# Low parts of the weights in the heads by an accumulating transfer instead of a VectorE subtraction

## The chip, the cores and the metric

The kernel runs on one core of a Trainium2 chip. The metric is the device time of one execution in microseconds (us). Five engines work side by side and meet through semaphores: TensorE (PE in the profile, with PEld for its weight loads), VectorE (DVE), ScalarE (ACT), GpSimd (POOL) and SyncE (SP). Transfers are issued by an engine's queue and carried out by 16 DMA engines; SP issues the plain weight loads, POOL issues those that add to what already lies in the destination.

## The reference, cut to what matters

The reference is a trunk of two residual layers on 512 tokens of width 1024. Each layer normalises x, multiplies it by one wide weight matrix, runs three token mixers on the pieces, gates and merges them and applies an output projection:

```python
for l in range(DEPTH):                                   # DEPTH = 2
    h = rms_norm(x, norm_gain[l])
    proj = jnp.einsum('bld,dn->bln', h, w_in[l])         # 1024 x 8448
    (qa, fa_f, fa_b, ia, za, ub, vb, zb, qc, kc, vc, zc,
     g_a, g_b, g_c) = jnp.split(proj, split_at, axis=-1)
    ya = hgrn2(qa, fa_f, fa_b, ia) ... * silu(za)        # 4 heads, both directions
    yb = spatial_gating(gelu(ub), gelu(vb), ...) * silu(zb)
    yc = window_attention(rope(qc), rope(kc), vc, ...) * silu(zc)
    merged = sigmoid(g_a) * (ya @ w_branch_a) + ...      # three branches
    x = x + merged @ w_out[l]
```

Everything is float32. The kernel computes a float32 product with TensorE's rounded type (fp32r) by splitting each operand into a high part (the value rounded to fp32r) and a low part (value minus high part), and adding three products: high x high, low x high, high x low. Every weight therefore needs a high and a low tile before TensorE can use it.

## The kernel before, in words

**Weights.** All weights are packed into tiles of 128 x 1024 float32 (512 KB). `weight_plan` gives 86 of them per layer in the order in which they are used: 14 tiles for the attention projections and the value IA of the recurrence; then the heads, which take tiles 14 to 41; then 36 tiles for the merges and 8 for the output projection. In layer 2 the same place has a number 92 higher among the operands, because the output projection makes 14 operands, some of them sums, from its 8 tiles, so that a layer has 92. This text writes #26 for operand 26. The stretch of the heads is, in this order: for head 0 the tiles QA, FF, FB, ZA (#14 to #17); the same for head 1 (#18 to #21); the four tiles of VB (#22 to #25); UB and ZB of group 0 and of group 1 (#26 to #29); heads 2 and 3 (#30 to #37); UB and ZB of groups 2 and 3 (#38 to #41).

**How a tile becomes an operand.** `w_load_to` loads it into one of four raw buffers (tag `wr`) through the SP queue (L207). `w_conv_to` takes a high buffer (tag `wh`, five of them) and a low buffer (tag `wl`, four of them) and calls `split`: ACT copies the raw tile into the high one, which rounds it (the CAST of L235), and DVE subtracts the high tile from the raw one into the low one (the TENSOR_TENSOR of L236). Only then can the raw buffer be loaded again. `w_ahead(n)` converts up to n operands ahead of the one in use and keeps the loads N_RAW ahead. In the output projection some raw tiles get a second tile added by a transfer from POOL (L209 and L230, `accum_op=ALU.add`); these are the only accumulating transfers.

**Who reads the operands.** A block of TensorE makes one 128 x 512 result in PSUM. `t_block` (L489) takes one tile with the weights as the stationary side: eight times the three products, so 24 matmuls that read the high tile first and the low tile third. `nat_block` (L442) has the activations stationary and reads four tiles at once: the VB stage runs over four blocks of 128 tokens, and each block reads all four VB tiles (units 0 to 3). So the four low buffers are all taken by VB's units until the last block of tokens has read them; the first low buffer to come free is unit 0's. (In the trace a t_block's matmul is written `pm<-hth,wl`, whichever side is stationary.)

**What sets the order.** The kernel is written as a main line of such blocks with side work (the recurrence `gla`, the attention, the spatial gate) put in between by `advance`. A scheduler then orders the instructions of each engine by its own model of their durations; only what is pinned stays in the order of the program. Each engine runs its list in order, and an instruction that waits holds up those behind it on its engine. The attention's score tiles pass through DRAM by POOL's transfers L781 (out) and L782 (back); gelu on VB's and UB's results is ACT's L1010 (Square) and L1013 (Sigmoid) with DVE's L1011, L1012 and L1014; L879 is an ACT copy inside the recurrence; L1031 is the side matmul in `ln_v` that multiplies a matrix of ones with the spatial weights.

Of the kernel before, what the change touches and what calls it, by code (L numbers as in the profile page):

```python
# [16 lines left out]
AF = mybir.ActivationFunctionType  # L17
ALU = mybir.AluOpType
# [16 lines left out]
C_QA, C_FF, C_FB, C_IA, C_ZA = 0, 512, 1024, 1536, 2048  # L35
# [14 lines left out]
def weight_plan():  # L50

    plan = []

    def nat(c):
        for i in range(4):
            plan.append(("n", c, i))

    nat(C_QC)
    for g in range(2):
        plan.append(("z", g))  # L60
    for i in range(2):
        plan.append(("k", C_KV, i))
    for g in range(2, 4):
        plan.append(("z", g))
    nat(C_IA)
    for h in range(H):
        for c in (C_QA, C_FF, C_FB, C_ZA):
            plan.append(("t", c + P * h))
        if h == 1:
            nat(C_VB)  # L70
        if h % 2 == 1:
            for g in (h - 1, h):
                plan.append(("t", C_UB + P * g))
                plan.append(("t", C_ZB + P * g))
    for br, cg in ((2, C_GC), (1, C_GB), (0, C_GA)):
        for n, j in enumerate(MERGE):
            plan.append(("t", cg + P * j))
            if n % 2 == 0:
                plan.append(("b", br, j, MERGE[n + 1]))

    for r, u in ((0, 0), (1, 0), (1, 1), (0, 1)):
        for i in range(2):
            plan.append(("o", u, 2 * r + i))
    return plan


PLAN = weight_plan()
NW = len(PLAN)

LOAD_SUM = {l * NW + NW - 2 + i: l * NW + NW - 4 + i for l in range(L) for i in range(2)}  # L90


def operand_plan():


    ops = []
    for l in range(L):
        ops += [(l * NW + k, None, None) for k in range(NW - 8)]
        x, w, z, y = ([l * NW + NW - 8 + 2 * q + i for i in range(2)] for q in range(4))
        t = [("sum", l, i) for i in range(2)]  # L100
        for a, b, c in ((x, y, None), (w, None, None), (x, None, (t, z)), (t, w, None), (z, None, None), (y, None, None), (t, None, None)):
            ops += [(a[i], b and b[i], c and (c[0][i], c[1][i])) for i in range(2)]
    return ops


OPERANDS = operand_plan()
# [3 lines left out]
def pack_weights(w_in, wa, wb, wc, wo):  # L110
    out = np.empty((L * NW, P, 1024), w_in.dtype)
    for l in range(L):
        wi = w_in[l].reshape(KT, P, -1)

        wcp = wc[l].reshape(2, 4, 64, D).transpose(1, 0, 2, 3)
        br = [w.reshape(4, P, D) for w in (wa[l], wb[l], wcp)]
        w2 = wo[l].reshape(KT, P, D)
        for i, it in enumerate(PLAN):
            if it[0] == "t":
                blk = wi[:, :, it[1] : it[1] + P]  # L120
            elif it[0] == "z":
                g = C_ZC + it[1] * 64
                blk = np.concatenate([wi[:, :, g : g + 64], wi[:, :, g + 256 : g + 320]], axis=2)
            elif it[0] == "k":
                blk = wi[4 * it[2] : 4 * it[2] + 4, :, it[1] : it[1] + 256]
            elif it[0] == "n":
                blk = wi[2 * it[2] : 2 * it[2] + 2, :, it[1] : it[1] + 512]
            elif it[0] == "b":
                w = br[it[1]]
                blk = np.concatenate([w[:, :, c * P : (c + 1) * P] for c in it[2:]], axis=0)  # L130
            else:
                blk = w2[2 * it[2] : 2 * it[2] + 2, :, it[1] * 512 : it[1] * 512 + 512]
            out[l * NW + i] = blk.transpose(1, 0, 2).reshape(P, 1024)
    return out
# [26 lines left out]
def build(nc, tc, cp, wp, sb, pp, dp, x, wpk, brow, gainb, pvec, wsp, trig, amask, imask, out):  # L161
    V, S, G, E = nc.vector, nc.scalar, nc.gpsimd, nc.tensor
# [4 lines left out]
    def nm(s):  # L167
        cnt[0] += 1
        return f"{s}_{cnt[0]}"

    def m4(shape=(P, 1024), dt=F32):
        return sb.tile(list(shape), dt, name=nm("m4"), tag="m4", bufs=N_M4)
# [23 lines left out]
    def w_load_to(i):  # L196
        while wstate["loaded"] < min(i, L * NW):
            k = wstate["loaded"]

            q = k % NW - (NW - 8)  # L200
            if q in (0, 1):
                if q == 0:
                    hold["t"] = sb.tile([P, 3, 1024], F32, name=nm("hold"), tag="scores", bufs=1)
                t = hold["t"][:, q]
            else:
                t = wp.tile([P, 1024], F32, name=nm("wr"), tag="wr", bufs=N_RAW)
            pin(nc.sync.dma_start(t, wpk[k]))  # L207
            if k in LOAD_SUM:
                G.dma_start(t, wpk[LOAD_SUM[k]], accum_op=ALU.add)  # L209
            raws[k] = t  # L210
            wstate["loaded"] += 1

    def raw(k):
        if k not in raws:
            w_load_to(k + 1)
        return raws[k]

    def w_conv_to(i, order=free, eng=V):
        while wstate["conv"] < min(i, len(OPERANDS)):
            n = wstate["conv"]  # L220
            k, add, form = OPERANDS[n]
            r = raw(k)
            if form:
                raws[form[0]] = hold["t"][:, 2] if form[0][2] == 0 else m4()
                G.tensor_tensor(raws[form[0]], r, raw(form[1]), ALU.add)
            hi = wp.tile([P, 1024], F32R, name=nm("wh"), tag="wh", bufs=N_HI)
            lo = wp.tile([P, 1024], F32R, name=nm("wl"), tag="wl", bufs=N_LO)
            split(r, hi, lo, order, eng)
            if add is not None:
                G.dma_start(r, wpk[add], accum_op=ALU.add)  # L230
            his[n], los[n] = hi, lo
            wstate["conv"] += 1

    def split(src, hi_dst, lo_dst, order=free, eng=V):
        order(S.copy(hi_dst, src))  # L235
        order(eng.tensor_tensor(lo_dst, src, hi_dst.bitcast(F32), ALU.subtract))  # L236

    wi = [0]

    def w_next():  # L240
        i = wi[0]
        wi[0] += 1
        w_conv_to(i + 1)
        return his[i], los[i]

    def w_ahead(n, eng=V):
        w_conv_to(wi[0] + n, eng=eng)
        n = min(wi[0] + n, len(OPERANDS) - 1)
        if n % NOPS >= NOPS - 14:
            w_load_to((n // NOPS + 1) * NW)  # L250
        else:
            w_load_to(OPERANDS[n][0] + N_RAW)
# [121 lines left out]
    s0 = pre.squares([0], 0, D, pin)  # L374
    pre.stats([0], s0, pin)
    w_conv_to(1, pin)
    pre.scale([0], pin, LO)
    pre.scale([0], pin, HI)
# [184 lines left out]
    for l in range(L):  # L563
# [27 lines left out]
        def nat_units(handler, us, before=None, two=False, passes=IN_ORDER):  # L591
            un = [w_next() for _ in range(4)]
            for tb in range(NT):
                if before is not None:
                    before(tb)
                if two and tb < 2:
                    if tb == 1:
                        pos = nat_two(un, *hN, (0, 1), lambda n: advance(us / 2))
                        for i in range(2):
                            handler(i, pos[i])  # L600
                            advance(us / 2)
                    continue
                po = nat_block(un, *hN, tb, lambda: advance(us), passes if tb == 0 else IN_ORDER)
                if tb == NT - 1:
                    w_ahead(2)
                handler(tb, po)
                advance(us)

        def nat_kv(handler, us):
            un = (w_next(), w_next())  # L610
            for pair in range(2):
                po = nat_pair(un, *hN, pair, lambda: advance(us))
                if pair == 1:
                    w_ahead(1)
                handler(pair, po)
                advance(us)

        def main_t():
            po = t_block(*w_next(), 0, *hT, KT, lambda: advance(2.6))
            w_ahead(1)  # L620
            return po
# [711 lines left out]
```

## Time and profile before

| | |
|---|---|
| time, median of 3 runs | 1082.95 us (1082.73 to 1083.31) |
| time of the profiled execution | 1083.25 us |
| its span in the trace | 1081.5 us |
| TensorE (PE) busy | 1073.6 us, 99% of the span |
| VectorE (DVE) busy | 743.6 us, 69% |
| ScalarE (ACT) busy | 439.9 us, 41% |
| GpSimd (POOL) busy | 75.8 us, 7% |
| read from HBM | 122.73 MB |
| heads of layer 1 in the trace | 89 to 294 us |
| heads of layer 2 in the trace | 621 to 825 us |

The span runs from the first to the last instruction in the trace; 1.75 us of the execution's time lie outside it. An engine is busy while an instruction of it runs; a queue's issuing work counts as busy for POOL only. Times on a row are from the span's start.

### The profile page before, as it was taken

To read this page: it belongs to the slowest core of one execution; us is meant where nothing else is said; L and a number is where in the kernel's file an instruction comes from. 1 tells how busy PE (TensorE), PEld (TensorE's weight loads), DVE (VectorE), ACT (ScalarE), POOL (GpSimd) and SP (SyncE) were. 2 spreads that over 40 slices of the span, in tenths; PEclk is the share of its full clock that TensorE was granted. 3 is DMA by queue.
4 is the path that set the end of the run, shared out by engine and by line. 5 is a ranking of instruction groups with operands and counts; after the bars stand their busy time and mean duration, and the time that the engine had idled before them with its cause. 6 is when DMAs were issued, how large, how long until landed. Compare 5 with 4: busy or idle time off the path is not lost.

```text
span 1081.5 us, 17209 instructions
## 1 busy us (share of the span) xinstructions
PE 1073.6 (99%) x6904; PEld 883.9 (82%) x6904; DVE 743.6 (69%) x1453; ACT 439.9 (41%) x673; POOL 75.8 (7%) x110
## 2 busy tenths in 40 slices
PE   9999999999999999999999999999999999999998
PEld 8888877878788888888879888687878888888886
DVE  6974799887974634356887578998688645335485
ACT  5354655354423423224534366554343223222342
POOL 0220111000000000001102201000000000000030
PEclk9999999999999999999999999999999999999999
DMA  8463454253223233244937345434413213323364
GB/s 307 151 200 108 156 176 157 76 193 108 75 64 98 78 98 98 95 138 91 299 127 229 122 157 191 140 118 153 140 43 96 63 71 101 98 79 120 115 178 132
DMA packets 40896, 141.67 MB, mean 131 GB/s; under 512 B 5104, under 2 KB 5616, under 8 KB 40816
## 3 DMA queue, kind: packets, MB, share of 16 engines
q1 hardware_dynamic: 28656, 100.20, 28.6%
q0 software_dynamic: 10432, 36.18, 11.9%
q10 hardware_dynamic: 1728, 4.20, 1.0%
q8 instruction: 54, 0.88, 0.3%
q14 instruction: 26, 0.21, 0.1%
HBM read 122.73 MB, written 17.83 MB: 130 GB/s over the span
## 4 chain that ended last, share of the span: by engine, by line
PE 97%; DVE 1%; ACT 1%; DMA 1%; issue 0%; SPq 0%; ACTq 0%
PE pm L489 65%; PE pm L442 11%; PE ps L1181 4%; PE pm L1181 4%; PE pm L477 2%; PE ps L795 2%; PE ps L890 1%; PE ps L980 1%; PE ps L745 1%; PE ps L746 1%; PE ps L987 1%; PE ps L970 1%; PE ps L939 1%; PE ps L1045 1%; DMA wr<-in_wpk 1%; PE ps L915 1%
## 5 line engine op out<-in xcount | busy, mean ns | idle before, releaser
L235 ACT CAST wh<-wr 128x1024 fp32r<-128x1024 f32 x168 | 176.4, 1053 | 389.8 <-PE pm L489 178.6
L489 PE MATMUL pm<-hth,wh 128*128 128x512 f32 x832 | 330.0, 397 | 0.0
L489 PE MATMUL pm<-htl,wh 128*128 128x512 f32 x832 | 325.1, 391 | 0.0
L489 PE MATMUL pm<-hth,wl 128*128 128x512 f32 x832 | 325.0, 391 | 0.0
L236 DVE TENSOR_TENSOR wl<-wr,wh 128x1024 fp32r<-128x1024 f32 x168 | 204.1, 1221 | 160.9 <-PE pm L489 103.9
L489 PEld LDWEIGHTS pm<-hth,wh 128*128 128x128 f32 x832 | 156.4, 188 | 33.9 <-issue 2.9
L489 PEld LDWEIGHTS pm<-hth,wl 128*128 128x128 f32 x832 | 156.3, 188 | 32.9
L489 PEld LDWEIGHTS pm<-htl,wh 128*128 128x128 f32 x832 | 156.5, 188 | 31.6 <-issue 1.3
L489 PE MATMUL pm<-m,wh 128*128 128x512 f32 x384 | 118.7, 391 | 0.0
L489 PEld LDWEIGHTS pm<-m,wh 128*128 128x128 f32 x384 | 71.8, 188 | 14.7
L948 DVE TENSOR_TENSOR m<-m,f 128x512 f32<-128x512 f32 x112 | 73.7, 687 | 7.2 <-PE ps L915 3.5
L442 PE MATMUL pm<-wh,hth 128*128 128x512 f32 x192 | 74.7, 398 | 0.6 <-ACT hth L235 0.5
L489 PE MATMUL pm<-m,wl 128*128 128x512 f32 x192 | 74.8, 390 | 0.0
L442 PE MATMUL pm<-wh,htl 128*128 128x512 f32 x192 | 73.6, 393 | 0.2 <-DVE htl L236 0.2
L442 PE MATMUL pm<-wl,hth 128*128 128x512 f32 x192 | 73.2, 392 | 0.0
L1124 DVE TENSOR_TENSOR t<-pm,t 128x512 f32<-128x512 f32 x32 | 22.1, 691 | 42.1 <-PE pm L489 42.1
L442 PEld LDWEIGHTS pm<-wh,hth 128*128 128x128 f32 x192 | 36.0, 188 | 10.2 <-ACT hth L235 1.3
L442 PEld LDWEIGHTS pm<-wh,htl 128*128 128x128 f32 x192 | 36.1, 188 | 7.7 <-DVE htl L236 0.5
L442 PEld LDWEIGHTS pm<-wl,hth 128*128 128x128 f32 x192 | 36.1, 188 | 7.5
L489 PEld LDWEIGHTS pm<-m,wl 128*128 128x128 f32 x192 | 36.1, 188 | 7.5
L230 POOL DMA_DIRECT2D hold<-in_wpk x6 | 5.3, 885 | 503.1 <-DVE wl L236 254.6
L879 ACT COPY t<-m 128x512 f32<-128x512 f32 x40 | 26.5, 679 | 23.0 <-DVE m L948 15.5
(205 smaller groups left out, 1430.8 us busy)
## 6 DMA issues: line engine op xcount, KB each, us to landing
wr<-in_wpk SPq DMA_DIRECT2D x168, 512.0 KB, 3.7
pd<-m POOLq DMA_DIRECT2D x20, 512.0 KB, 3.8
m<-pd POOLq DMA_DIRECT2D x20, 512.0 KB, 4.8
m<-in_x SPq DMA_DIRECT2D x8, 512.0 KB, 7.2
m<-xd POOLq DMA_DIRECT2D x16, 256.0 KB, 6.6
hold<-in_wpk POOLq DMA_DIRECT2D x6, 512.0 KB, 5.8
xd<-t POOLq DMA_DIRECT2D x8, 256.0 KB, 3.6
hold<-in_wpk SPq DMA_DIRECT2D x4, 512.0 KB, 4.9
```

Source lines behind the costliest of these rows:

```text
L235: order(S.copy(hi_dst, src))
L236: order(eng.tensor_tensor(lo_dst, src, hi_dst.bitcast(F32), ALU.subtract))
L442: E.matmul(po, a, b[:, o : o + 512], start=first and n == 0, stop=last and n == len(passes) - 1)
L477: E.matmul(po[:, k, :], a, b[:, o : o + 256], start=n == 0, stop=n == 23)
L489: E.matmul(po, s, m, start=n == 0, stop=n == 3 * nk - 1)
L745: E.matmul(sp[:, :nk], qt[qb][:, h, :], ktt[0][:, g, k0 * P : k1 * P], start=True, stop=False)
L746: E.matmul(sp[:, :nk], qt[qb][:, h, :], ktt[1][:, g, k0 * P : k1 * P], start=False, stop=True)
L795: E.matmul(po[64 * g : 64 * g + 64], vC[:, k0 + kb, 64 * g : 64 * g + 64], pt[:, :, 128 * g : 128 * g + 128], start=kb == 0, stop=kb == le ...
L879: S.copy(kx.rearrange("p (g b m) -> p g b m", b=2, m=m), custom(kd, 0, ([2 * m, nb // 2], [T + m, 2], [1, m])))
L948: V.tensor_tensor(v, v, custom(ff, of, ([sd, 2], [2, ng], [0, m])), ALU.mult)
L1124: V.tensor_tensor(sg, po, sg, ALU.mult)
L1181: E.matmul(banks[g], get(a, kt, g), b[:, o : o + 512], start=not onto and kt == 0 and n == 0, stop=kt == 3 and n == 2, skip_group_check=on ...
```

## The change

The change concerns 23 of the 86 tiles of each layer, 46 in all: the weights of the heads that are used as `t` tiles, but for the very first (#15 to #21 and #26 to #41, and the same in layer 2; not #14 and not VB's four). For these `split` is not called. ACT makes the high tile as before (now L232). ACT then writes the negative of the rounded tile into the low buffer (L233: Identity with scale -1, stored in the rounded type), and POOL issues a transfer that reads the raw 512 KB from HBM a second time and adds them to it (L234). What comes out is value minus high part, as before. DVE's subtraction is gone for them. In `w_ahead` the conversions run at least two operands ahead when the operand in turn is one of these. Below line 246 the changed kernel's line numbers are 11 higher than before's: L489 is L500, L442 is L453, L879 is L890, L1010 and L1013 are L1021 and L1024, L1031 is L1042, L781 and L782 are L792 and L793.

```diff
+BY_DMA = [PLAN[k][0] == 't' and PLAN.index(('t', C_QA)) < k < NW - 44 for k in range(NW)]
...
             hi = wp.tile([P, 1024], F32R, name=nm("wh"), tag="wh", bufs=N_HI)
             lo = wp.tile([P, 1024], F32R, name=nm("wl"), tag="wl", bufs=N_LO)
-            split(r, hi, lo, order, eng)
+            if isinstance(k, int) and BY_DMA[k % NW]:
+
+                S.copy(hi, r)
+                S.activation(lo, r, AF.Identity, scale=-1.0)
+                G.dma_start(lo, wpk[k], accum_op=ALU.add)
+            else:
+                split(r, hi, lo, order, eng)
...
     def w_ahead(n, eng=V):
+        k = OPERANDS[min(wi[0], len(OPERANDS) - 1)][0]
+        if isinstance(k, int) and BY_DMA[k % NW]:
+            n = max(n, 2)
         w_conv_to(wi[0] + n, eng=eng)
```

On the engines, DVE loses 46 subtractions, ACT gains 46 activations and 6 loads of its function tables (ACT_TABLE_LOAD, 19 before and 25 now), POOL gains 46 issues, and SP's list keeps its length.

ACT around the end of the VB stage of layer 1, in the kernel before. `wh_309` is the high tile of #27 and the next ones are those of #28 to #30; the L1010 and L1013 rows are VB's gelu, L879 the recurrence:

```order
L879 COPY t2_303_1775<-m4_194_1072 128x512
L1013 ACTIVATE m4_299_1726<-m4_299_1726 128x512
L235 CAST wh_309_1818<-wr_308_1816 128x1024
L235 CAST wh_341_1965<-wr_311_1822 128x1024
L879 COPY t2_305_1798<-m4_233_1293 128x512
L235 CAST wh_350_2046<-wr_312_1824 128x1024
L1010 ACTIVATE m4_299_1726<-pm_301_1739 128x512
```

The same place in the changed kernel, with the negated copies of #26 (`wl_307`), #27 (`wl_310`), #28 (`wl_331`) and #29 (`wl_345`):

```order
L890 COPY t2_303_1782<-m4_197_1080 128x512
L1024 ACTIVATE m4_299_1733<-m4_299_1733 128x512
L233 ACTIVATE wl_307_1820<-wr_258_1403 128x1024
L232 CAST wh_309_1826<-wr_308_1824 128x1024
L890 COPY t2_305_1805<-m4_236_1305 128x512
L233 ACTIVATE wl_310_1827<-wr_308_1824 128x1024
L232 CAST wh_330_1918<-wr_311_1831 128x1024
L233 ACTIVATE wl_331_1919<-wr_311_1831 128x1024
L1021 ACTIVATE m4_299_1733<-pm_301_1746 128x512
L232 CAST wh_344_1981<-wr_312_1833 128x1024
```

`wl_307` was made by DVE before; now ACT makes its negated copy right behind the gelu of the third token block, ahead of the CAST of #27, and each later CAST has such a copy of its own beside it.

POOL at the same place in the changed kernel (before, only the L781 and L782 rows, then so numbered, stood there):

```order
L792 DMA pd_298_1718<-m4_297_1716 128x1024
L234 DMA wl_307_1820<-in_wpk 128x1024
L793 DMA m4_297_1716<-pd_298_1718 128x4x256
L234 DMA wl_310_1827<-in_wpk 128x1024
L792 DMA pd_316_1846<-m4_315_1844 128x1024
L234 DMA wl_331_1919<-in_wpk 128x1024
L234 DMA wl_345_1982<-in_wpk 128x1024
L793 DMA m4_315_1844<-pd_316_1846 128x4x256
```

The accumulating transfers stand between the two halves of the attention's trip through DRAM, in one list with them.

PE at the end of the VB stage of layer 2, where the first UB block (#118: `wh_1069`, `wl_1070`) begins, before:

```order
L442 MATMUL pm_1062_6438<-wl_1043_6200,hth_763_4773 128x512
L489 MATMUL pm_1079_6540<-hth_763_4773,wh_1069_6516 128x512
L489 MATMUL pm_1079_6540<-htl_764_4774,wh_1069_6516 128x512
L489 MATMUL pm_1079_6540<-hth_763_4773,wl_1070_6517 128x512
L489 MATMUL pm_1079_6540<-hth_763_4773,wh_1069_6516 128x512
```

and in the changed kernel:

```order
L453 MATMUL pm_1062_6468<-wl_1043_6230,hth_763_4796 128x512
L500 MATMUL pm_1079_6572<-hth_763_4796,wh_1069_6546 128x512
L500 MATMUL pm_1079_6572<-htl_764_4797,wh_1069_6546 128x512
L1042 MATMUL ps_1088_6612<-ws_947_5735,ones_96 128x512
L500 MATMUL pm_1079_6572<-hth_763_4796,wl_1070_6547 128x512
L500 MATMUL pm_1079_6572<-hth_763_4796,wh_1069_6546 128x512
```

The side matmul L1042 (L1031 before), which stood after twelve matmuls of this block, now stands ahead of the first read of `wl_1070`.

On ACT, at that place of layer 2, the negated copy of #118 comes behind a CAST of #119 (`wh_1072`) and a gelu:

```order
L890 COPY t2_1058_6428<-m4_997_6027 128x512
L232 CAST wh_1072_6553<-wr_1071_6551 128x1024
L1024 ACTIVATE m4_1060_6455<-m4_1060_6455 128x512
L233 ACTIVATE wl_1070_6547<-wr_1019_6125 128x1024
L890 COPY t2_1066_6509<-m4_958_5802 128x512
L233 ACTIVATE wl_1073_6554<-wr_1071_6551 128x1024
```

Before, the CAST of #119 came behind that gelu (then L1013). Now it stands ahead of it, and the negated copy of #118 comes behind both.

## The prediction

> **What bounds the kernel now.** I read the page's engines and its chain first, then the heads' stretches by themselves, since an average over the span hides stages.
>
> ```profile
> span 1081.5 us, 17209 instructions
> PE 1073.6 (99%) x6904; PEld 883.9 (82%) x6904; DVE 743.6 (69%) x1453; ACT 439.9 (41%) x673; POOL 75.8 (7%) x110
> PEclk9999999999999999999999999999999999999999
> PE 97%; DVE 1%; ACT 1%; DMA 1%; issue 0%; SPq 0%; ACTq 0%
> ```
>
> TensorE is busy 99% of the span, holds 97% of the chain that ends last, and is granted its full clock in all 40 slices. The next view counts busy time in the heads of layer 1 and layer 2, where all 46 changed tiles are used.
>
> ```profile
> core 0: us, PE busy (x) PEld busy (x) DVE busy (x) ACT busy (x) POOL busy (x), PEclk, DMA share, GB/s
> 89.00:294.00 205.00, 204.66 (x1708) 163.18 (x1707) 173.62 (x392) 107.57 (x190) 13.26 (x20) 1.00 0.42 135
> 621.00:825.00 204.00, 203.75 (x1703) 162.12 (x1702) 172.04 (x385) 105.38 (x188) 13.32 (x20) 1.00 0.40 131
> ```
>
> DVE is 85% busy there, yet TensorE idles only 205.00 - 204.66 = 0.34 us and 204.00 - 203.75 = 0.25 us. Whatever is taken off DVE in the heads can therefore win at most 0.6 us. Could TensorE itself run quicker with a calmer DVE? The chain has one long run of matmuls in the merges:
>
> ```profile
> 360.27 146.92 PE pm L489 x648
> ```
>
> 146.92 / 648 = 0.2267 us from start to start. In the heads, two starts of layer 2 quoted below (710.34 and 712.38, nine matmuls apart) give 2.04 / 9 = 0.2267 too. The rate is the same with DVE busy or not, so there is no gain to be had from it.
>
> **The change, part by part.** What the edits take from one engine and give to others is priced by these groups (before the bar: busy us, mean ns; behind it: idle time before):
>
> ```profile
> L236 DVE TENSOR_TENSOR wl<-wr,wh 128x1024 fp32r<-128x1024 f32 x168 | 204.1, 1221 | 160.9 <-PE pm L489 103.9 <-issue 50.5 <-PE pm L477 4.1
> L345 ACT ACTIVATE m<-m 128x1024 f32<-128x1024 f32 x4 | 4.2, 1058 | 2.8 <-DMA m<-in_x 2.8
> L763 ACT ACT_TABLE_LOAD x6 | 7.7, 1283 | 0.1
> L230 POOL DMA_DIRECT2D hold<-in_wpk x6 | 5.3, 885 | 503.1 <-DVE wl L236 254.6 <-DVE m L1125 248.5
> ```
>
> - DVE: 46 x 1.221 = 56.2 us less. It lies under TensorE's work; worth 0 to 0.6 us, and I take 0.
> - ACT: 46 negated copies, priced by the activation of the same shape, 46 x 1.058 = 48.7 us, and 6 table loads, 6 x 1.283 = 7.7 us. ACT was busy 107.57 + 105.38 = 213 of 409 us in the heads and would be at 269: hidden as a sum, not wherever one copy comes late.
> - POOL: 46 x 0.885 = 40.7 us of issuing, on 26.6 of 409 us: hidden as a sum.
> - HBM: 46 x 0.5 MB more through DMA engines at 0.40 to 0.42 busy: hidden as a sum.
>
> What is not a sum is the **latency of one tile**. Before, 1.22 us of DVE led from a free low buffer to a low tile. Now it is a copy on ACT, an issue on POOL and a whole transfer. It cannot start sooner, because the negated copy writes the low buffer itself, and so waits until TensorE has last read what the buffer held, four operands back. For most tiles that is a block or more of TensorE's work ahead, and the latency is covered. It is not covered for the first block behind VB (#26, and #118 in layer 2): VB's four units hold all four low buffers until its last block of tokens. The rows of layer 1 (start, duration):
>
> ```profile
> 173.52 0.39 PE L442 MATMUL pm<-wl,hth 128*128 128x512 f32 x1
> 178.79 0.39 PE L489 MATMUL pm<-hth,wh 128*128 128x512 f32 x1
> 179.25 0.39 PE L489 MATMUL pm<-hth,wl 128*128 128x512 f32 x1
> 172.75 0.64 ACT L1013 ACTIVATE m<-m 128x512 f32<-128x512 f32 x1
> 169.97 1.24 DVE L777 STREAM_TRANSPOSE m<-scores 128x1024 f32<-128x1024 f32 x1
> 171.51 0.56 POOL L781 DMA_DIRECT2D pd<-m  x1 [1.15 <-DVE m L777]
> ```
>
> Unit 0's low tile is last read by the matmul of 173.52, done at 173.91. ACT is through its gelu (L1013) at 173.39, and by the changed order the copy of #26 is next, so it runs from about 173.95 to 175.0. From a producer's end to POOL's issue takes 171.51 - (169.97 + 1.24) = 0.30 us, so the transfer is issued at 175.3. TensorE wants the low tile at 179.25. With L for the time from issue to landing, the stall is 175.3 + L - 179.25 = **L - 3.95 us**.
>
> Layer 2, PE first and then ACT:
>
> ```profile
> 704.39 0.39 PE L442 MATMUL pm<-wh,htl 128*128 128x512 f32 x1
> 710.34 0.39 PE L489 MATMUL pm<-hth,wl 128*128 128x512 f32 x1
> 712.38 0.39 PE L489 MATMUL pm<-hth,wl 128*128 128x512 f32 x1
> 712.61 1.02 PE L1031 MATMUL ps<-ws,ones 128*128 128x512 f32 x2
> 713.70 0.40 PE L489 MATMUL pm<-htl,wh 128*128 128x512 f32 x1
> 703.61 0.63 ACT L1013 ACTIVATE m<-m 128x512 f32<-128x512 f32 x1 [1.25 <-DVE m L1012]
> 704.82 1.06 ACT L235 CAST wh<-wr 128x1024 fp32r<-128x1024 f32 x1 [0.57 <-PE pm L442]
> ```
>
> Here the changed order puts the CAST of #119 ahead, and it needs unit 0's high buffer, read until 704.78; as before it runs from 704.82 to 705.87. Then come the gelu (its 0.63 us overlap their neighbours a little, 0.54 is my estimate) to 706.41, the copy of #118 to 707.46 and the issue at 707.76. In TensorE's favour the side matmul L1031 now stands ahead of the first low read. It put the next L489 pair off from 712.61 to 713.70, 1.09 us, so the low tile is wanted at 710.34 + 1.09 = 711.43. The stall is **L - 3.67 us**.
>
> For **L** the trace has POOL's accumulating transfers of the same 512 KB in the output projection (issue ns and landing us, min/median/max), and the plain loads:
>
> ```profile
> L230 POOL DMA_DIRECT2D hold<-in_wpk x6: 850/884/919, 493.4 to 1050.6; - x6
> DMA to landing us min/median/max: 5.3/6.8/10.8
> wr<-in_wpk SPq DMA_DIRECT2D x168, 512.0 KB, 3.7
> hold<-in_wpk POOLq DMA_DIRECT2D x6, 512.0 KB, 5.8
> ```
>
> L is bounded below by 3.7 (a plain load) and above by 10.8. The traffic at the two places and at the accumulating transfers between 513.8 and 540.8 us, and what runs beside the one of #26:
>
> ```profile
> 173.00:182.00 9.00, 9.00 (x101) 7.03 (x100) 8.32 (x16) 5.85 (x8) 1.25 (x2) 1.00 0.65 234
> 704.00:715.00 11.00, 11.00 (x108) 8.52 (x107) 10.69 (x22) 6.21 (x8) 0.75 (x1) 1.00 0.66 230
> 513.80:540.80 27.00, 26.87 (x122) 22.02 (x121) 24.27 (x41) 14.65 (x20) 5.00 (x4) 1.00 0.94 299
> 175.90 0.75 POOL L782 DMA_DIRECT2D m<-pd  x1 [3.84 <-DMA pd<-m]
> 176.32 3.03 SPq L207 DMA_DIRECT2D wr<-in_wpk  x2
> ```
>
> At 0.65 the DMA engines are busy, but not swamped as at 0.94, where the long landings were. I take the middle of the two medians, 5.8 (page) and 6.8 (with the two that go to another buffer): **L = 6.3**. The stalls are 2.35 and 2.63, in all **5.0 us**.
>
> Nothing else is as tight. #15 (head 0's second tile) is next:
>
> ```profile
> 92.94 0.39 PE L442 MATMUL pm<-wl,hth 128*128 128x512 f32 x1
> 93.30 1.05 ACT L235 CAST wh<-wr 128x1024 fp32r<-128x1024 f32 x1
> 103.73 0.39 PE L489 MATMUL pm<-hth,wl 128*128 128x512 f32 x1
> ```
>
> Its buffer is free at 93.33, ACT behind the CAST at 94.35, the copy ends at 95.4, the issue is at 95.7, and with 6.3 it lands at 102.0 against 103.73: covered by 1.7 us, as long as L stays under 8.0. The lookahead of two lets the later tiles start early enough that only the buffers hold them. The attention's transfers wait behind the new issues for under 1 us each, and nobody waits for them that closely.
>
> The sum, 0 + 0 + 5.0, is made against the profiled execution: 1081.5 + 1.75 outside the span = 1083.25, then 1088.2. That execution is 0.3 us above the median 1082.95, so the forecast is 1082.95 + 5.0 = **1087.9 us**. With L from 5.3 to 6.8 the likeliest case alone reaches from 3.0 to 6.0 us, 1085.9 to 1088.9.
>
> On issuing there is a rule that speaks against the change. The Trainium skill ("SBUF — State Buffer", section "SBUF: two separate sides") says that POOL's descriptors cannot be written while DVE runs an operation that takes both of its ports. The trace does not agree so far: the L230 issues lie between 850 and 919 ns although DVE was busy 24.27 of 27 us around some of them.
>
> **The rivals.** *No measurable change:* the accumulating transfer is as quick as a plain load in the heads. The two stalls sum to 2L - 7.6, which is below 0.2% (2.17 us, about what a measurement of this kernel can tell from no change) when L is under 4.9; at L = 3.7 both are gone, 1083.0. For it speaks the lighter traffic, against it that no accumulating transfer in the trace landed under 5.3. Chance 0.20.
>
> *Crowded transfers:* raw loads, attention and accumulations meet, and L grows past 6.8. Half way to the maximum, at 8.8, the stalls are 4.85 + 5.13 = 10.0, 1093; at 10.8 they are 14.0, 1097, and #15 adds 95.7 + 10.8 - 103.73 = 2.8. For it speaks the share of 0.65 before anything is added, against it that the long landings stand at 0.94. Chance 0.14.
>
> *DVE's relief pays:* its side work comes sooner and TensorE's gaps close; that decides only if the stalls are covered (L below 3.7). It can win 0.6 us by the heads' rows, 1082.4; more would need idle time of TensorE that the view does not show. Chance 0.06, of which 0.04 for a gain beyond the 0.2%.
>
> *A pause costs clock:* if TensorE slowed to half speed for a block after each stall, 24 x 0.2267 = 5.4 us come on top of each, 5.0 + 10.9, 1098.8. The PEclk row never falls below full speed, but it has no pause of that length in it either. The Trainium skill ("TensorE: Matmul & The Clock Gate", Part 1) puts such a slowing behind idle windows of about 3.4 us. Chance 0.03.
>
> *Issues wait for DVE:* if each issue first waited for DVE's running operation, at most 1.24 us (L777) at each stall, the sum is 5.0 + 2.5, 1090.4. The issue times above speak against it; it is the skill's rule named above. Chance 0.03.
>
> **How the numbers follow.** The forecast of two stalls keeps 0.54. Faster by over 0.2%: 0.04. Within: 0.20 + 0.02 = 0.22. Slower: 0.54 + 0.14 + 0.03 + 0.03 = 0.74. The range goes from 1082.8, which takes in no change, to 1092.5, which takes in half of the crowded case; the rest of that, a clocked-down TensorE and a real gain are left out.
>
> **What would show it.** Right: two idle stretches of TensorE of 1.3 to 2.9 us at the third matmul of the first L500 block behind VB, near 179 and 714 us, put down to a transfer into `wl`, with a landing of 5.3 to 6.8 us behind each, and the rest of the heads as tight as before; DVE's busy time down by 56 us with nothing won. Wrong: no such gaps (landing under 4.9), gaps at many blocks (the buffers, ACT or POOL's list bind more often than I counted), a longer matmul rate in the heads, or a granted clock under 1.00 after a gap.

## The result and the profile after

The changed kernel takes **1099.84 us** (1098.74 to 1100.96, 4 runs) against 1082.87 us: a ratio of 1.0155, 95% interval 1.0142 to 1.0168. That is 17 us slower; 5 us were forecast, and the range ended at 1092.5. The profiled execution took 1100.34 us, its span is 17.1 us longer than before's.

The page of the changed kernel: span, engines, granted clock, the chain by engine, and the new transfers with their median landing.

```profile
span 1098.6 us, 17266 instructions
PE 1079.3 (98%) x6904; PEld 886.0 (81%) x6904; DVE 694.2 (63%) x1407; ACT 489.8 (45%) x725; POOL 116.3 (11%) x156
PEclk9999998999999999999999999989999999999999
PE 89%; DMA 4%; issue 3%; DVE 3%; ACT 1%; POOL 0%; SPq 0%; ACTq 0%; POOLq 0%
wl<-in_wpk POOLq DMA_DIRECT2D x46, 512.0 KB, 8.2
```

DVE lost 49 us, ACT and POOL gained 50 and 41 (priced at 56, 56 and 41). What is new is a DMA share of 4% on the chain (1% before) and two slices with a lowered clock. The list of waits names one culprit for TensorE (in total, times, longest):

```profile
PE pm L500 <- DMA wl<-in_wpk: 10.7, 4, 6.2
```

Layer 1, behind the VB stage (PE, then ACT, POOL and SP; a bracket gives the idle time before the row and what ended it):

```profile
179.56 0.39 PE L500 MATMUL pm<-htl,wh 128*128 128x512 f32 x1
183.92 0.79 PE L500 MATMUL pm<-hth,wl 128*128 128x512 f32 x1 [3.98 <-DMA wl<-in_wpk]
184.51 0.63 PE L500 MATMUL pm<-hth,wh 128*128 128x512 f32 x1
184.94 0.63 PE L500 MATMUL pm<-htl,wh 128*128 128x512 f32 x1
189.88 0.39 PE L500 MATMUL pm<-htl,wh 128*128 128x512 f32 x1
174.53 1.06 ACT L233 ACTIVATE wl<-wr 128x1024 fp32r<-128x1024 f32 x1 [0.67 <-PE pm L453]
175.89 0.89 POOL L234 DMA_DIRECT2D wl<-in_wpk  x1 [3.36 <-ACT wl L233]
175.62 2.75 SPq L209 DMA_DIRECT2D wr<-in_wpk  x2
```

The low tile is issued at 175.89 and wanted one step behind 179.56, at 179.79: 3.90 us, where the prediction had 3.95. But TensorE can go on only at 183.92, 8.03 us after the issue. And then its steps are 0.43 us (184.51 to 184.94) in place of 0.23. Layer 2:

```profile
718.41 0.39 PE L500 MATMUL pm<-htl,wh 128*128 128x512 f32 x1
718.64 1.02 PE L1042 MATMUL ps<-ws,ones 128*128 128x512 f32 x2
725.81 0.79 PE L500 MATMUL pm<-hth,wl 128*128 128x512 f32 x1 [6.16 <-DMA wl<-in_wpk]
726.40 0.63 PE L500 MATMUL pm<-hth,wh 128*128 128x512 f32 x1
731.95 0.41 PE L500 MATMUL pm<-htl,wh 128*128 128x512 f32 x1
714.63 1.04 ACT L233 ACTIVATE wl<-wr 128x1024 fp32r<-128x1024 f32 x1
715.98 0.89 POOL L234 DMA_DIRECT2D wl<-in_wpk  x1 [0.87 <-ACT wl L233]
```

Wanted at 718.64 + 1.09 = 719.73, 3.75 us after the issue (3.67 forecast), and had at 725.81, 9.83 us after it. The two stretches as windows; the last three numbers are granted clock, DMA share and GB/s:

```profile
179.00:191.00 12.00, 8.02 (x23) 5.58 (x22) 5.89 (x16) 4.84 (x6) 2.73 (x5) 0.72 1.05 262
719.00:733.00 14.00, 7.84 (x21) 5.65 (x20) 6.51 (x21) 4.51 (x7) 3.48 (x4) 0.63 1.04 295
```

The sum of the loss, from these rows:

| | layer 1 | layer 2 |
|---|---|---|
| pause | 183.92 - 179.79 = 4.13 | 725.81 - 719.73 = 6.08 |
| half clock after it | (189.88 - 183.92) - 3.36 = 2.60 | (731.95 - 725.81) - 14 x 0.2267 = 2.97 |

The 3.36 us are what the same stretch (low matmul to the matmul behind the side work) takes at full clock in layer 2 of before, 710.34 to 713.70. Together 15.8 of 17.1 us. Of the rest, 0.54 us are two short waits for #15 and its twin (0.18 us at 104.1 and 0.36 at 642.95), and the remainder are small differences in the order that I have not followed up.

### The profile page after: what moved, and what is told of

The parts are those of the page before. It is cut to its first block, busy times and chain, and to the rows that moved or that the text cites. A ratio compares the mean times of both kernels' runs of the same rounds, so it can differ in the third digit from the quotient of the medians.

```text
span 1098.6 us, 17266 instructions
## 1 busy us (share of the span) xinstructions
PE 1079.3 (98%) x6904; PEld 886.0 (81%) x6904; DVE 694.2 (63%) x1407; ACT 489.8 (45%) x725; POOL 116.3 (11%) x156
## 4 chain that ended last, share of the span: by engine, by line
PE 89%; DMA 4%; issue 3%; DVE 3%; ACT 1%; POOL 0%; SPq 0%; ACTq 0%; POOLq 0%
PE pm L500 63%; PE pm L453 6%; PE ps L1192 4%; PE pm L1192 3%; DMA wl<-in_wpk 3%; PE pm L488 2%; PE ps L806 1%; PE ps L991 1%; PE ps L901 1%; PE ps L756 1%; PE ps L757 1%; PE ps L998 1%; PE ps L981 1%; PE ps L950 1%; PE ps L1056 1%
## 5 line engine op out<-in xcount | busy, mean ns | idle before, releaser
L500 PE MATMUL pm<-hth,wl 128*128 128x512 f32 x832 | 326.9, 393 | 10.7 <-DMA wl<-in_wpk 10.7
L500 PE MATMUL pm<-hth,wh 128*128 128x512 f32 x832 | 331.0, 398 | 0.0
L500 PE MATMUL pm<-htl,wh 128*128 128x512 f32 x832 | 326.3, 392 | 0.0
L244 DVE TENSOR_TENSOR wl<-wr,wh 128x1024 fp32r<-128x1024 f32 x122 | 148.1, 1219 | 128.9 <-PE pm L500 75.6
L500 PEld LDWEIGHTS pm<-hth,wl 128*128 128x128 f32 x832 | 157.3, 189 | 46.0 <-DMA wl<-in_wpk 12.8
L500 PEld LDWEIGHTS pm<-hth,wh 128*128 128x128 f32 x832 | 157.4, 189 | 33.6 <-issue 2.1
L500 PEld LDWEIGHTS pm<-htl,wh 128*128 128x128 f32 x832 | 157.5, 189 | 32.6 <-issue 1.9
L500 PE MATMUL pm<-m,wh 128*128 128x512 f32 x384 | 118.6, 390 | 0.0
L500 PEld LDWEIGHTS pm<-m,wh 128*128 128x128 f32 x384 | 71.8, 188 | 14.8
L232 ACT CAST wh<-wr 128x1024 fp32r<-128x1024 f32 x46 | 48.2, 1047 | 73.9 <-PE pm L500 42.1
L453 PE MATMUL pm<-wh,hth 128*128 128x512 f32 x192 | 74.8, 399 | 0.6 <-ACT hth L243 0.5
L500 PE MATMUL pm<-m,wl 128*128 128x512 f32 x192 | 74.7, 389 | 0.0
L453 PE MATMUL pm<-wh,htl 128*128 128x512 f32 x192 | 73.5, 392 | 0.2 <-DVE htl L244 0.2
L453 PE MATMUL pm<-wl,hth 128*128 128x512 f32 x192 | 73.3, 392 | 0.0
L234 POOL DMA_DIRECT2D wl<-in_wpk x46 | 40.2, 894 | 198.0 <-ACT wl L233 185.2
L233 ACT ACTIVATE wl<-wr 128x1024 fp32r<-128x1024 f32 x46 | 48.5, 1059 | 0.7 <-PE pm L453 0.7
L758 DVE CUSTOM_DVE_ANT_0 scores<-ps,am,rows 128x256 f32<-128x256 f32 (+1 forms) x64 | 32.2, 545 | 21.6 <-PE ps L757 21.6
L453 PEld LDWEIGHTS pm<-wh,hth 128*128 128x128 f32 x192 | 36.0, 188 | 10.3 <-ACT hth L243 1.3
```

Source lines behind the costliest of these rows:

```text
L232: S.copy(hi, r)
L233: S.activation(lo, r, AF.Identity, scale=-1.0)
L234: G.dma_start(lo, wpk[k], accum_op=ALU.add)
L453: E.matmul(po, a, b[:, o : o + 512], start=first and n == 0, stop=last and n == len(passes) - 1)
L500: E.matmul(po, s, m, start=n == 0, stop=n == 3 * nk - 1)
L758: V.tensor_tensor_reduce(sm[:, :nkb, h, :], sp[:, :nk].rearrange("p (k t) -> p k t", t=P), amv, rq[1][:, 8 * qb + h : 8 * qb + h + 1], NEG ...
```

## The experiments

The theory at the outset: the loss is the wait at one place per layer, the first block behind VB, and the half clock that follows it. The rival: the extra work of ACT, POOL and the DMA engines costs all over the heads. Edits are shown against the changed kernel unless said otherwise; times are medians, with the 95% interval of the ratio to the kernel before where it decides.

**Which tiles.**

```diff
 x26_29:  BY_DMA = [... < NW - 44 and not 26 <= k <= 29 for k in range(NW)]
 x26:     BY_DMA = [... < NW - 44 and k != 26 for k in range(NW)]
 only26:  BY_DMA = [k == 26 for k in range(NW)]
```

x26_29. 

> The changed kernel, but the four tiles behind VB (#26 to #29 and their twins in layer 2) keep VectorE's subtraction; 38 of 46 tiles still go by the accumulating transfer. Theory of one place (the loss is the wait for the low tile of the first block behind VB, and half clock after that pause): both pauses vanish, PEclk 1.00 everywhere, 1083 within 1.5 us, although DVE has still lost 38 subtractions (46 us). Rival of a spread loss (ACT's, POOL's and the DMA engines' extra work in the whole of the heads, by the number of tiles): 38/46 of the 17 us stay, 1097.

only26. 

> Only #26 and its twin go by the accumulating transfer, 2 of 46. Theory of one place with landings made long by the neighbours (#27 to #29 are issued 2.4, 4.3 and 6.7 us behind #26): the landing of #26 alone is 5.7 to 6.5 us, as the lone ones of the changed kernel; two pauses of 2 to 2.8 us, too short to lower the granted clock: 1087 to 1088.5. If the landing is as long without neighbours (8 to 9.8): two pauses of 4 to 6 us with half clock behind them, about 1099. Rival of a spread loss: 2/46 of 17 us, 1083.6.

x26. 

> All but #26 and its twin go by the accumulating transfer. Theory of one place: the wait passes to the next block. In the changed kernel #27 was issued at 178.3 and landed 10.7 us later at 189.0; without a pause ahead it is wanted 24 matmuls after #26's, at 185.8. With one transfer fewer ahead of it, landing in 8 to 9.5: pauses of 0.5 to 2 us per layer, no loss of clock, 1084 to 1087. If only #26 itself matters: 1083. Rival of a spread loss: 44/46 of 17, 1099.

Measured: x26_29 **1099.34** (ratio 1.012 to 1.016), only26 **1096.24** (1.010 to 1.013), x26 **1099.69** (1.014 to 1.017; its profile is of a quicker execution, span 1093.5). So two tiles of 46 already cost 13 us, which rules out the rival of a spread loss. But taking the four tiles behind VB out saves nothing, which rules out "one place" too. In x26_29 TensorE now waits elsewhere; its longest wait is for a tile of head 2 in layer 2 (ACT, POOL, PE):

```profile
739.49 2.00 ACT L233 ACTIVATE wl<-wr 128x1024 fp32r<-128x1024 f32 x2
740.84 1.82 POOL L234 DMA_DIRECT2D wl<-in_wpk  x2 [22.99 <-ACT wl L233]
749.75 0.80 PE L500 MATMUL pm<-hth,wl 128*128 128x512 f32 x1 [3.93 <-DMA wl<-in_wpk]
```

Here ACT was not waiting for a buffer: its row has no idle time ahead of it, the copy stood in ACT's list behind a table load and the softmax of the attention. Start to use is again 10 us: copy 1.05, issue 0.30, landing 8.9. The theory has to be wider: **a tile of this kind is late wherever the order leaves it less than about 10 us**, and the stall moves to the next such tile when one is taken out (x26: 1.74 us at #27 in layer 1, 6.6 in layer 2). only26 shows in addition that the long landing does not need the other accumulating transfers.

**Why the landing is long.** The negated copy is the last reader of the raw tile. When it ends, SP starts the next plain load into that buffer, ahead of the accumulating transfer: 175.62 against 175.89 in the rows above. So the tile's own copy puts a rival load beside it. Made from the high tile, the copy does not hold the raw buffer:

```diff
-                S.activation(lo, r, AF.Identity, scale=-1.0)
+                S.activation(lo, hi.bitcast(F32), AF.Identity, scale=-1.0)
```

neghi_only26 (only #26 and its twin). 

> As only26 (only #26 and its twin by the accumulating transfer), but ACT makes the negated copy from the high tile, not from the raw one. The raw buffer is then free after the CAST, and its next plain load no longer starts with the copy, 0.27 us ahead of the transfer. Theory that this load makes the landing long: 5.7 to 6.5 us in place of 7.8 and 8.8, pauses of 1.8 to 2.8 us, no half clock, 1086.5 to 1088. Rival (the accumulating transfer is that slow by itself in the heads, or by the attention's transfers): landings near 8, 1095 to 1096 as only26.

neghi (all 46). 

> The changed kernel with all negated copies made from the high tile, so no transfer of the 46 starts together with the plain load that its own copy released. If these loads make the landings long: median landing 6 to 7 in place of 8.2, #26 at 6 to 7.5 since #27 to #29 still follow; pauses of 2 to 3.5 us, clock lost at most once, 1087 to 1093. If the accumulating transfers hold each other up: landings of 8 and more remain, 1096 to 1100.

Measured: neghi_only26 **1091.61**, 4.6 us less than only26; neghi **1097.82**. Layer 1 of only26, then of neghi_only26:

```profile
175.13 4.30 SPq L209 DMA_DIRECT2D wr<-in_wpk  x2
175.41 0.90 POOL L234 DMA_DIRECT2D wl<-in_wpk  x1 [3.26 <-ACT wl L233]
183.26 0.50 PE L500 MATMUL pm<-hth,wl 128*128 128x512 f32 x1 [3.76 <-DMA wl<-in_wpk]
```

```profile
175.29 0.90 POOL L234 DMA_DIRECT2D wl<-in_wpk  x1 [3.31 <-ACT wl L233]
178.93 0.33 SPq L209 DMA_DIRECT2D wr<-in_wpk  x1
181.27 0.50 PE L500 MATMUL pm<-hth,wl 128*128 128x512 f32 x1 [1.99 <-DMA wl<-in_wpk]
```

Issue to use falls from 7.85 to 5.98 us where the load is no longer released by the copy, as forecast for that layer. In layer 2 another load still came 0.6 us behind the transfer; the pause fell from 5.42 to 3.85 us, but stayed longer than expected. With all 46 (neghi) the gain is small, against the expectation: the median landing is 8.0 us, the pauses are 3.97 and 5.35. In layer 1 of neghi a plain load is again issued close to the tile's transfer, 0.66 us behind it (176.44 against 175.78), and the transfers of #27 to #29 follow; these two are not separated there. So half of the theory holds: where the load is gone, the landing is some 2 us shorter, but a copy from the high tile does not keep loads away when all 46 tiles are made so.

plain. 

> The changed kernel with the same 46 transfers from POOL at the same places, but plain: they overwrite the low tile with the raw weights and add nothing (the low parts are so left out; the result of the kernel is another). It measures what the adding costs. Theory that the addition makes the transfer longer: landing of 4 to 6 us, pauses under 2 us, 1083 to 1087. Rival (POOL's queue and the traffic make it, added or not): landings of 8 and more, 1096 to 1100.

```diff
-                G.dma_start(lo, wpk[k], accum_op=ALU.add)
+                G.dma_start(lo, wpk[k])
```

Measured **1091.63**. The landing's median falls from 8.2 to 5.8 us, and the issue takes less time; the pause in layer 1 is shorter by 1.4 us (2.58 for 3.98), but not gone:

```profile
wl<-in_wpk POOLq DMA_DIRECT2D x46, 512.0 KB, 5.8
182.02 0.80 PE L500 MATMUL pm<-hth,wl 128*128 128x512 f32 x1 [2.58 <-DMA wl<-in_wpk]
```

Neither side had it: adding accounts for some 2.4 us of a median landing. What is left above the 3.7 us of a plain load from SP in the kernel before, some 2.1 us, is the crowd or POOL's queue; this run does not separate them.

**More time.** `late` lets the blocks of these 46 tiles take the low tile last (`late` is true for them alone):

```diff
-    def t_block(wh, wl, o, mvh, mvl, nk, mid=None):
+    def t_block(wh, wl, o, mvh, mvl, nk, mid=None, late=False):
...
-            for s, m in ((a, mvh(kt)), (a, mvl(kt)), (b, mvh(kt))):
-                E.matmul(po, s, m, start=n == 0, stop=n == 3 * nk - 1)
...
+        passes = [(kt, j) for kt in range(nk) for j in range(3)]
+        if late:
+            passes = [(kt, j) for kt in range(nk) for j in range(2)] + [(kt, 2) for kt in range(nk)]
+        for kt, j in passes:
...
+            w = (wl if j == 2 else wh)[:, o + kt * P : o + (kt + 1) * P]
+            E.matmul(po, w, (mvl if j == 1 else mvh)(kt), start=n == 0, stop=n == 3 * nk - 1)
```

> The changed kernel with the same transfers, but in the blocks of these tiles TensorE does the 16 matmuls on the high tile first and the 8 on the low tile last, so the low tile is wanted 14 matmuls (3.2 us) later. Theory of one place: pauses 4.1 - 3.2 = 0.9 and 6.1 - 3.2 = 2.9 us, both too short to lower the granted clock, so the 5.6 us of half clock go too: 1082.9 + 3.8 = 1086.7, up to 1088. If the clock is lost for another reason than the length of the pause, 5 us more, 1092. Rival of a spread loss: no change, 1099.8.

Measured **1093.05** (1.008 to 1.011): 7 of the 17 us are gone. In layer 1 the pause is 2.10 us, and no clock is lost; in layer 2 it is still 5.2 us (2.9 expected). In both layers the landing had grown to over 9 us.

`nlo5` takes a fifth low buffer, and gives up a work tile:

```diff
-N_RAW, N_HI, N_LO = 4, 5, 4
+N_RAW, N_HI, N_LO = 4, 5, 5
...
-N_M4, N_T2, N_PM, N_PS = 19, 7, 3, 5
+N_M4, N_T2, N_PM, N_PS = 18, 7, 3, 5
```

> The changed kernel with five low buffers in place of four (and 18 work tiles in place of 19, for the room). Theory (the chain copy, issue, landing starts only when VB's units give a low buffer back): #26 gets a buffer that head 1 leaves, starts some 8 us sooner, and has no pause; #27 now takes the first buffer of VB, wanted 5.8 us later than #26, with a landing of 8 to 10 a pause of 0 to 2.5 us per layer: 1083 to 1089. Rival (the transfers are short of bandwidth, and an earlier start doesn't help): pauses of 4 us and more remain, 1094 to 1100.

Measured **1091.34**. #26 has no pause in either layer, as expected; in layer 1 there is none at all. In layer 2 the next tile is 4.31 us late, with half clock behind, more than forecast. Two covers, `neghi_late`, and all three, `late_nlo5_neghi`:

> Two of the three covers: negated copies from the high tile and low tiles read last, but four low buffers and 19 work tiles as in the changed kernel. In the changed kernel with the high-tile copies the pauses were 3.97 and 5.35 us, both with half clock. Theory of time (wanted 3.2 us later): 0.8 and 2.2, clock lost at most once: 1083 + 3.0 = 1086, up to 1088.5. Rival (the fifth buffer was what helped, the rest doesn't add): 1091 to 1093, as with late reads alone.

> The changed kernel with three covers at once: low tiles read last in their blocks (3.2 us), five low buffers in place of four (18 work tiles for the room), negated copies made from the high tile. Theory (a pause is copy + issue + landing minus the time from free buffer to first read): with five buffers one pause of 4.3 us was left, in layer 2; 3.2 us later wanted, it is about 1.1 and costs no clock; 1.9 us were lost elsewhere with 18 work tiles: 1083 + 1.1 + 1.9 = 1086, 1084 to 1088. Rival (bandwidth, not time, is short): 1090 or more, as each cover alone.

Measured **1090.59** and **1085.00** (1.0008 to 1.0028). With all three no wait of TensorE for `wl` is left in the trace; the longest one is outside the heads:

```profile
PE ps L1195 <- DVE sl L244: 1.6, 1, 1.6
```

With two, layer 1 is at 0.73 us, but layer 2 still pauses for 5.5. The rows of `neghi_late` there (ACT, POOL, PE) show another term:

```profile
707.34 1.06 ACT L233 ACTIVATE wl<-wh 128x1024 fp32r<-128x1024 f32 x1
711.24 0.82 POOL L796 DMA_DIRECT2D m<-pd  x1 [5.18 <-PE pm L453]
712.04 2.73 POOL L234 DMA_DIRECT2D wl<-in_wpk  x3
720.55 0.79 PE L501 MATMUL pm<-hth,wl 128*128 128x512 f32 x1 [5.50 <-DMA wl<-in_wpk]
```

The copy is done at 708.40, and POOL issues the transfer only at 712.04. Ahead of it in POOL's list stands the attention's transfer back from DRAM (L796), itself waiting until 711.24. Taken off POOL:

```diff
-                G.dma_start(pt, pd.rearrange("(a j) b n -> (j b) a n", j=32))
+                nc.sync.dma_start(pt, pd.rearrange("(a j) b n -> (j b) a n", j=32))
```

> As neghi_late, but the attention's transfers back from DRAM are issued by SP, not by POOL. In neghi_late POOL issued #118's transfer 3.64 us after its copy had ended, because such a transfer back stood ahead of it in POOL's list and waited for its way out to land. Theory: that wait goes from #118's path; its pause of 5.5 us falls to about 2, without half clock: 1090.6 - 3.6 - 2.5 = 1084.5, 1083 to 1087. Rival (the landing, 8.5 us, decides and grows when the transfer starts sooner among the others): 1089 to 1091.

Measured **1093.95** (1092.05 to 1100.57). The wait for `wl` did fall, from 6.2 to 2.6 us in all, and #118 has no pause any more (issued at 711.02, landed 5.5 us later). But the total rose, against both sides of the expectation. In the trace the attention's transfer now stands in SP's list ahead of the plain weight loads, four of which leave within 2 us behind it (from 712.62 on); ACT waits 4 us for a raw tile, and what TensorE waits for now comes late behind ACT and DVE (SP, ACT, then the waits):

```profile
700.26 12.31 SPq L796 DMA_DIRECT2D m<-pd  x3
712.62 17.15 SPq L209 DMA_DIRECT2D wr<-in_wpk  x9
719.27 1.05 ACT L232 CAST wh<-wr 128x1024 fp32r<-128x1024 f32 x1 [4.03 <-DMA wr<-in_wpk]
PE pm L501 <- DMA wl<-in_wpk: 2.6, 2, 1.7
PE ps L759 <- DVE sm L307: 1.7, 1, 1.7
PE ps L759 <- DVE sm L761: 1.3, 1, 1.3
```

**The other parts of the change.** `look2` is the kernel before with the lookahead of two alone:

```diff
+        k = OPERANDS[min(wi[0], len(OPERANDS) - 1)][0]
+        if isinstance(k, int) and PLAN[k % NW][0] == 't' and PLAN.index(('t', C_QA)) < k % NW < NW - 44:
+            n = max(n, 2)
```

> The kernel before with the other edit alone: in the heads the conversions run at least two operands ahead, low parts still by VectorE. Theory (only the time from copy to landing costs): no pause, 1083 within 1 us. Rival (the earlier conversions disturb the order and the buffers, and part of the 17 us is theirs): 1085 or more.

`nosub` has no low part for the 46 tiles (in the branch of BY_DMA `lo = hi` replaces the copy and the transfer):

> The changed kernel without any low part for the 46 tiles: no subtraction, no negated copy, no transfer; TensorE reads the high tile twice (so the low parts are left out of the result; TensorE's work is the same). It measures alone what VectorE's relief of 56 us can be worth. By the bound of TensorE's idle time in the heads: 0 to 0.6 us, 1082.4 to 1083. Rival (a calmer VectorE lets the side work come sooner and shortens more than the heads): 1080 or less.

Measured: look2 **1082.22** (ratio 0.9983 to 1.0002), nosub **1083.02** (0.9990 to 1.0009). The lookahead costs nothing. Without the subtractions, and with nothing in their place, DVE is 50 us less busy and TensorE does the same work:

```profile
PE 1072.4 (99%) x6904; PEld 882.8 (82%) x6904; DVE 693.0 (64%) x1407; ACT 447.4 (41%) x679; POOL 75.8 (7%) x110
```

That the time does not move is the direct measure of what the change could win: nothing above 0.1%.

**Controls for the five buffers.** The kernel before with 18 work tiles, and with five low buffers besides:

> The kernel before with 18 work tiles in place of 19 and nothing else. If the 1.9 us that the version with three covers loses at about 521 us, behind the merges, comes from the missing work tile: 1085 within 0.5, with a wait of TensorE for VectorE's split of the sums there. If it comes from the accumulating transfers: 1083.

> The kernel before with five low buffers and 18 work tiles, no accumulating transfer for low parts. If the 1.9 us near 521 (TensorE waits for VectorE's split of a sum) come with the five buffers and the order they lead to: 1085, with that wait in the trace. If they come from the accumulating transfers of the heads: 1084.3, as with 18 work tiles alone, and no such wait.

Measured **1084.27** (1.0003 to 1.0023) and **1088.15** (1.0033 to 1.0063). Both cost something by themselves: 1.3 us for the missing work tile, without the wait that was looked for, and 5.3 us with the five buffers, more than either side expected. The wait near 521 us is there with the five buffers and no accumulating transfer, once in each layer:

```profile
PE ps L1181 <- DVE sl L236: 3.2, 2, 1.6
```

So the 1.6 us that the three covers leave come with the buffers and the order of work they lead to, not with the transfers. Why `late_nlo5_neghi` has that wait in one layer only, and is 3 us faster than its control, I did not test.

## Why the prediction was wrong

**What held.** TensorE bounds the kernel, and DVE's relief is worth nothing: forecast 0 to 0.6 us, measured 0 (nosub). ACT's, POOL's and HBM's extra work is hidden as a sum. The places were right, the first block behind VB in both layers, and so were the times from issue to first read: 3.95 and 3.67 forecast, 3.90 and 3.75 measured. #15, called covered as long as L stays under 8.0, landed 8.42 us after its issue in layer 1 and was late by 0.18 us there and 0.36 in layer 2; #16 to #21 were covered.

**The step that failed: L.** The sum took L = 6.3 us from issue to landing; it was 8.03 and 9.83 (to the waiting matmul). The view of all 46 landings:

```profile
L234 POOL DMA_DIRECT2D wl<-in_wpk x46: 841/862/1489, 95.6 to 816.2; - x46
DMA to landing us min/median/max: 5.7/8.2/15.2
```

The error was to read the crowd from the kernel before. I took 6.3, the middle of two medians, because the DMA share at both places was 0.65 and not 0.94. No transfer of the kernel before landed in such a time: of its twelve accumulating transfers of weights, six took 5.3 to 5.8 us and six 7.8 to 10.8. And the change itself brings the crowd: the copy's end starts a plain load, and three more accumulations follow. Three traces show what each counts for (layer 1, layer 2; us):

| | issue to use | DMA share meanwhile |
|---|---|---|
| changed kernel | 8.03, 9.83 | 0.90, 0.96 |
| only26: the other accumulations gone | 7.85, 8.80 | 0.85, 0.88 |
| neghi_only26: the load that the copy releases gone too | 5.98, 7.19 | 0.74, 0.79 |

So the other accumulations count for 0.2 and 1.0 us, the load for 1.9 and 1.6. Without both, layer 1 is inside the 5.3 to 6.8 that I gave to L; in layer 2 another load is still beside the transfer. With the measured L the terms give 4.08 + 6.16 = 10.2 us, the value of the rival of crowded transfers (10.0), which had 0.14.

**The second failure: rivals counted as if they excluded each other.** The other 5.6 us are the clock, given 0.03. But a clock that falls after a pause is not another cause beside crowded transfers, it follows from them: the longer the landing, the likelier the drop. Together the two rivals make 1082.95 + 10.0 + 10.9 = 1103.8, and with the clock's measured size 1098.6. Its size was taken too high: 24 matmuls at half speed, 5.4 us per pause, where about 14 steps were slow, 2.6 to 3.0 us.

**How long a pause may be.** The runs hold many pauses with the granted clock behind each. Three windows, the granted clock third from the end: behind 2.12 us (x26_29), 2.58 us (plain) and 3.76 us (only26).

```profile
224.00:230.00 6.00, 5.07 (x22) 4.22 (x23) 5.00 (x13) 2.86 (x4) 0.85 (x1) 1.00 1.05 264
181.00:188.00 7.00, 5.98 (x18) 4.50 (x19) 3.23 (x10) 2.28 (x3) 0.53 (x1) 0.76 1.01 350
182.00:188.00 6.00, 4.74 (x13) 3.48 (x13) 1.10 (x3) 0.63 (x1) 0.30 (x1) 0.72 0.64 242
```

Of the pauses of TensorE in these traces, all fourteen from 2.58 to 6.6 us cost clock. Of the six from 1.7 to 2.2 us five did not and one did, in neghi_late_sp: it went on at 723.15, and the clock fell about a microsecond later.

```profile
723.15 0.36 PE L759 MATMUL ps<-m,m 128*128 128x256 f32 x1 [1.73 <-DVE sm L307]
724.00:728.00 4.00, 4.00 (x13) 3.18 (x13) 3.66 (x17) 4.00 (x6) 1.71 (x2) 0.57 0.90 222
```

So the length of the pause alone does not decide. Where it lies matters too: in these traces the granted clock changes only at borders 3.41 us apart, and each of the fifteen stretches at half clock that belong to these pauses lasts 3.41, 6.83 or 10.24 us. In eleven of them the clock fell before the pause was over. In layer 1 of the changed kernel, the step that holds most of the pause, the stretch at half clock and the step behind it:

```profile
178.99:182.41 3.42, 0.95 (x5) 0.45 (x3) 3.42 (x9) 3.39 (x5) 1.67 (x3) 1.00 1.03 220
182.41:189.23 6.82, 5.31 (x12) 3.82 (x13) 1.34 (x4) 1.46 (x2) 0.88 (x1) 0.50 1.05 293
189.23:192.64 3.41, 3.41 (x15) 2.63 (x14) 2.78 (x12) 0.25 (x1) 0.79 (x1) 1.00 1.06 216
```

In layer 1 of `late` a border, at 183.47, divides the pause of 2.10 us, and no clock is lost:

```profile
180.06:183.47 3.41, 2.86 (x11) 1.69 (x9) 3.41 (x12) 2.38 (x3) 0.86 (x1) 1.00 1.04 253
183.47:186.88 3.41, 1.87 (x8) 1.56 (x9) 1.53 (x9) 0.95 (x1) 0.00 (x0) 1.00 1.06 247
```

The first number behind the length is TensorE's busy time. Cut at these borders from 100 to 1060 us, every step at full clock with 1.36 us or less of it was followed by half clock, and none with 1.79 or more; of the three between, two kept the clock (1.56 and 1.67) and that of neghi_late_sp lost it (1.69). The Trainium skill ("TensorE: Matmul & The Clock Gate", Part 1) names idle windows of about 3.4 us. The traces agree with that length, but the step need not be idle throughout: pauses of 2.58 and even 1.73 us were enough here. At the forecast stalls of 2.35 and 2.63 us the clock was already at stake, and 0.03 was far too little.

**The issue rule.** The issues took 841 to 1489 ns, 862 in the median, with DVE busy 63% of the span, so no general hold-up by DVE shows in them. The rule I weighed ("SBUF — State Buffer", "SBUF: two separate sides", of the Trainium skill) concerns DVE operations that take both of its ports; which of this kernel's do, no run here shows. What did hold issues up was POOL's own list (neghi_late: 3.64 us), which the prediction put at under 1 us, and in the other direction.

**What stays open.** Times differ from execution to execution (x26: 1095.2 to 1101.2 us), and of each kernel one execution was traced, so the shares of the neighbours above are differences of single landings. What the attention's transfers add to a landing was not tested: in layer 1 of all three traces one is issued 0.6 us behind the tile, in layer 2 they lie differently. The share of the clock was read from traces, not set by an experiment. Of the last 1.3 us of the loss, 0.8 have no place.

## What to carry to other kernels

A step that moves from an engine into a transfer trades busy time for latency: first find each operand's time from the moment its buffer is free to its first read, and compare it with copy, issue and landing together, here about 10 us against a subtraction of 1.2. Take the landing from a stretch as crowded as the change will make it, and ask what the new instruction's end sets free. Where the bound engine would pause for some 2 us or more, add the price of its clock: here it was half as much again.

## What the runs showed of the hardware

- An accumulating transfer of 512 KB lands in 5.7 us at best, in 8.2 in the median and in up to 15.2 in the changed kernel; the same as a plain transfer from POOL has a median of 5.8, and its issue takes 0.53 to 0.62 us in place of 0.86.
- TensorE's granted clock fell to half (steps of 0.43 in place of 0.23 us) at every pause of 2.58 us and more, and at one of six from 1.7 to 2.2 us. It changed only at borders 3.41 us apart, and was at half for one to three such steps; whether it fell went by how long TensorE was busy in the step before (1.36 us or less: always; 1.79 or more: never).
- An issue's time grew from 862 ns in the median to 1489 for the last of three accumulating issues in a row.
